# A ring of eight output banks for an MLP, and three instructions of a norm moved behind the next half's sum

## The chip, the cores and the metric

The kernel runs on one core of a Trainium2 chip. The metric is the time of one execution on the device in microseconds; a measurement is the median of several runs.

The engines are TensorE (in the profile PE for products and PEld for loading their weights), VectorE (DVE), ScalarE (ACT), GpSimd (POOL) and the queues that issue transfers. TensorE leaves its results in PSUM, the output memory. It has eight banks, and a product group adds up in one of them until VectorE or ScalarE has read it out.

## The reference, cut to what matters

One inference step of a two-layer decoder trunk on 512 prompt tokens and 8 x 4 sample tokens, in float32. Layer 0 mixes with an mLSTM and a GLA head group, layer 1 with a Mamba-2 SSD mixer; the change touches neither of these two.

```python
def _layernorm(x, g, b):
    xf = x.astype(jnp.float32)
    mu = xf.mean(-1, keepdims=True)
    var = jnp.square(xf - mu).mean(-1, keepdims=True)
    y = (xf - mu) * lax.rsqrt(var + LN_EPS) * g.astype(jnp.float32) + b.astype(jnp.float32)
    return y.astype(x.dtype)

def _mlp(x, w1, w2):
    return jnp.square(jax.nn.relu(x @ w1)) @ w2

for l in range(DEPTH):                      # DEPTH = 2, D_MODEL = 1024, D_FF = 4096
    mix, ... = _ab_mixer(x, ...) if l % 2 == 0 else _ssd_mixer(x, ...)
    x = _layernorm(DN_ALPHA * x + mix, P['ln_mix_g'][l], P['ln_mix_b'][l])
    x = _layernorm(DN_ALPHA * x + _mlp(x, P['mlp_w1'][l], P['mlp_w2'][l]), P['ln_mlp_g'][l], P['ln_mlp_b'][l])
```

## The kernel before, in words

**Layout.** All 544 tokens run together, with features on the 128 partitions and tokens along the free axis: 1024 features are eight tiles (`KT`), the tokens two halves of 272 (`TH`; `hf` is 0 or 1). The stages run in the order `ab`, `mlp0`, `ssd`, `mlp1`, each mixer followed by its output projection, and each projection and each MLP by a norm. The residual stream of a half is `xf[hf]`.

**Products.** A float32 operand is split in a high part (`xh`, `whi`, `hh`, made by ScalarE) and the low remainder (`xl`, `wlo`, `hlo`, made by VectorE). Each 128x128 block of weights takes three products of 272 columns: high by high, high by low, low by high. `dense` (products at L362) adds up one group: one output tile of 128 features for one half, over `kt` blocks, 3 x `kt` products in one bank. Then the evacuation `evac` is issued with high priority. `residual` (L394, L396) is the evacuation that adds a bank to `xf` on VectorE.

**The MLP.** Of the 32 tiles of hidden features the first six (`HEADM`) are dense groups of 24 products. The other 26 are made by `pair`, two tiles for both halves at a time, with seven quarter products instead of eight (Strassen's scheme in Winograd's form): `quarter` issues 12 products at L508, so a pair has 84. A pair uses four banks, of which three are read out and then added to again in the later quarters. The order of pairs and output blocks is the written-out list `MLP`: two output blocks of hidden tiles 0 to 5 (`n` = 6: groups of 18 products), two of hidden tiles 6 and 7 (`n` = 2: eight groups of six products each), then two for every four hidden tiles (eight groups of 12), with a pair after each, and at the end one block of hidden tiles 24 to 31 (`n` = 8).

**Banks before.** There are two sources. `psd` is a pool of three banks, taken in turn; all dense groups use it. `pm` gives the other five, in turn (outside of the SSD layer). A pair takes two from each. The norms' sums over features, `mu` (L420) and `var` (L431), take theirs from `pm`.

**The norm.** `layernorm` runs once for each half, spread between the products: it is a generator in the lane "norm", and each product issued ticks the lane's first generator, which yields how many products it lets pass first (the numbers in `W`). The steps of a half: the sum of its eight tiles of `xf` is made as they are evacuated (L403, L405: on VectorE for the first half; for the second half on GpSimd, the last of them on VectorE). A product with ones makes the mean of it (L420); VectorE removes it (L423), ScalarE squares (L424), VectorE adds the squares up (L425 to L428). Another product makes the variance (L431), ScalarE the reciprocal root (L433, L434). Then for each of eight tiles VectorE scales (L441), ScalarE writes the high part `xh` (L442), VectorE the low part `xl` (L443). Last, ScalarE adds the bias to `xf` in place (L445). The first half's norm runs while TensorE makes the second half's last seven or eight groups of the stage before; the second half's norm while TensorE makes the next stage's first groups, which begin with the first half. A generator behind another in the same lane waits until that one has ended.

**Order on the engines.** TensorE's instructions stand in the order in which the program issues them. For the other engines a planner simulates the kernel's time and lays out each engine's queue ahead of the run, by priority and by when it believes an instruction to be ready. Weight splits (L166 on ScalarE, L167 on VectorE; in the pairs L202, L203) and evacuations have high priority. `tc.issue_after(i)` keeps instructions behind `i` in the queue of `i`'s engine.

**After the first MLP** the SSD layer's first five groups are computed ahead, `xf` is written to memory by GpSimd's queue ("spill") and read again later.

## Time and profile before

| what | value |
| --- | --- |
| median of 3 runs | 1516.64 us (1515.93 to 1519.11) |
| the profiled execution | 1513.8 us, its span 1512.1 us |
| mean granted TensorE clock in the profile | 0.996 |
| `ab` with its projection, to 304 us | TensorE busy 299.06 of 304.00 us |
| `mlp0`, 304 to 678 us | TensorE busy 371.24 of 374.00 us |
| `ssd` with its projection, 678 to 1130 us | TensorE busy 438.45 of 452.00 us |
| `mlp1`, from 1130 us | TensorE busy 369.29 of 382.10 us |

The span is the time from the first to the last instruction in the trace; the rest of the execution lies around it. The times of the views below are microseconds from the span's start. A row of the timeline has start, duration, engine, line, operation, output and inputs, shapes and count, and in brackets the idle time of the engine before it with what ended it.

### The profile page before, as it was taken

What the parts mean: (1) busy time and instruction counts of PE and PEld (TensorE: products, weight loads), DVE (VectorE), ACT (ScalarE), POOL (GpSimd) and SP (SyncE); (2) the same over time, 40 slices, a digit from 0 to 9 for tenths busy, and PEclk for the clock granted to TensorE, in tenths of its full rate; (3) what the DMA queues carried; (4) which work ended last, traced back from release to release, by engine and by line L of the source; (5) the groups of instructions that cost most, each with busy time, mean ns of one, the idle gap of its engine ahead of it and who ended that gap; (6) DMA issues with size and microseconds to landing.
All of it is one profiled execution on the core that took longest, in us unless ns stands there. A gap on an engine that the chain in (4) does not pass through costs nothing.

```text
span 1512.1 us, 29214 instructions
## 1 busy us (share of the span) xinstructions
PE 1478.0 (98%) x11637; PEld 1426.0 (94%) x11637; DVE 1097.9 (73%) x2067; ACT 794.4 (53%) x1748; POOL 230.4 (15%) x295
## 2 busy tenths in 40 slices
PE   9999999999999999999999999999999999999997
PEld 9999989999999999999888789899999999999996
DVE  4956676786776766678898988776688677676656
ACT  5645556573543443447875675554257354344333
POOL 0511221100000000024444354420010000000000
PEclk9999999999999999999999999999999999999999
DMA  6321325223322332433556766364222332233121
GB/s 227 93 68 57 116 85 147 73 71 95 98 90 93 98 87 68 154 128 130 134 178 195 243 169 222 104 211 132 71 74 70 97 96 89 93 99 97 57 85 60
DMA packets 88369, 172.11 MB, mean 114 GB/s; under 512 B 9240, under 2 KB 43928, under 8 KB 87976
## 3 DMA queue, kind: packets, MB, share of 16 engines
q1 hardware_dynamic: 55256, 140.09, 29.7%
q10 hardware_dynamic: 30192, 19.41, 4.8%
q0 software_dynamic: 2784, 10.75, 1.8%
q8 instruction: 91, 1.49, 0.4%
q14 instruction: 46, 0.38, 0.1%
HBM read 153.48 MB, written 16.73 MB: 113 GB/s over the span
## 4 chain that ended last, share of the span: by engine, by line
PE 85%; DVE 6%; ACT 3%; DMA 3%; issue 1%; POOL 1%; ACTq 0%; DVEq 0%; POOLq 0%
PE psd L362 58%; PE psd L508 17%; DMA E<-d_cs 1%; PE num L758 1%; PE yp L1573 1%; PE gs L984 1%; DVE wlo L167 1%; ACT whi L166 1%; PE sp L1551 1%; PE it L1620 1%; DVE xf L396 1%; PE ip L1548 1%; DVE acc L1467 1%; DVE xl L443 1%; PE sps L1627 0%
## 5 line engine op out<-in xcount | busy, mean ns | idle before, releaser
L362 PE MATMUL psd<-xh,whi 128*128 128x272 f32 x1504 | 446.5, 297 | 2.5 <-ACT ci L1457 2.3
L362 PE MATMUL psd<-xh,wlo 128*128 128x272 f32 x1504 | 441.1, 293 | 0.5 <-DVE wlo L167 0.5
L362 PE MATMUL psd<-xl,whi 128*128 128x272 f32 x1504 | 438.3, 291 | 0.2 <-DVE xl L282 0.2
L362 PE MATMUL psd<-hh,whi 128*128 128x272 f32 x1024 | 297.0, 290 | 3.6 <-DVE xf L396 2.5
L362 PE MATMUL psd<-hlo,whi 128*128 128x272 f32 x1024 | 295.5, 289 | 0.2
L362 PE MATMUL psd<-hh,wlo 128*128 128x272 f32 x1024 | 295.2, 288 | 0.0
L362 PEld LDWEIGHTS psd<-xh,whi 128*128 128x128 f32 x1504 | 284.3, 189 | 10.0 <-issue 5.1
L362 PEld LDWEIGHTS psd<-xl,whi 128*128 128x128 f32 x1504 | 284.9, 189 | 5.9 <-issue 4.2
L362 PEld LDWEIGHTS psd<-xh,wlo 128*128 128x128 f32 x1504 | 284.1, 189 | 4.7 <-issue 2.8
L167 DVE TENSOR_TENSOR wlo<-wraw,whi 128x1024 fp32r<-128x1024 f32 (+2 forms) x173 | 206.7, 1196 | 58.4 <-ACT whi L166 57.3
L166 ACT CAST whi<-wraw 128x1024 fp32r<-128x1024 f32 (+2 forms) x173 | 174.2, 1011 | 132.2 <-PE psd L362 114.7
L362 PEld LDWEIGHTS psd<-hh,whi 128*128 128x128 f32 x1024 | 192.8, 188 | 5.7 <-DVE xf L396 4.4
L362 PEld LDWEIGHTS psd<-hlo,whi 128*128 128x128 f32 x1024 | 192.7, 188 | 0.8 <-DVE hlo L282 0.6
L362 PEld LDWEIGHTS psd<-hh,wlo 128*128 128x128 f32 x1024 | 192.7, 188 | 0.1
L396 DVE TENSOR_TENSOR xf<-xf,psd 128x272 f32<-128x272 f32 x208 | 87.9, 432 | 77.3 <-PE psd L362 76.7
L508 PE MATMUL psd<-xh,whi 128*128 128x272 f32 x416 | 120.2, 289 | 0.9 <-DVE xf L396 0.9
L508 PE MATMUL psd<-xh,wlo 128*128 128x272 f32 x416 | 119.9, 288 | 0.0
L508 PE MATMUL psd<-xl,whi 128*128 128x272 f32 x416 | 119.6, 288 | 0.0
L202 ACT CAST whi<-wsum 128x1024 fp32r<-128x1024 f32 x52 | 54.3, 1044 | 120.9 <-PE psd L508 72.0
L202 ACT CAST whi<-wraw 128x1024 fp32r<-128x1024 f32 (+1 forms) x52 | 43.4, 834 | 96.6 <-PE psd L362 85.3
L203 DVE TENSOR_TENSOR wlo<-wsum,whi 128x1024 fp32r<-128x1024 f32 x52 | 63.6, 1224 | 23.1 <-ACT whi L202 23.1
L508 PEld LDWEIGHTS psd<-xh,whi 128*128 128x128 f32 x416 | 78.2, 188 | 1.6 <-DVE xf L396 1.4
(468 smaller groups left out, 2826.5 us busy)
## 6 DMA issues: line engine op xcount, KB each, us to landing
wraw<-mlp_w SPq DMA_DIRECT2D x80, 512.0 KB, 3.6
wraw<-ssd_in SPq DMA_DIRECT2D x40, 512.0 KB, 3.9
wraw<-mlp_w SPq DMA_DIRECT2D x64, 256.0 KB, 2.9
wraw<-ab_in SPq DMA_DIRECT2D x24, 512.0 KB, 3.6
h<-h SPq DMA_DIRECT2D x32, 256.0 KB, 4.4
h0n<-h0n SPq DMA_DIRECT2D x16, 512.0 KB, 4.4
E<-d_cs ACTq DMA_DIRECT2D x16, 512.0 KB, 4.3
s_h<-h0n POOLq DMA_DIRECT2D x16, 512.0 KB, 4.5
```

The costliest lines, as they stand in the source:

```text
L166: nc.scalar.copy(hi[:, r], w[:, r])
L167: nc.vector.tensor_tensor(lo[:, r], w[:, r], hi[:, r].bitcast(F32), ALU.subtract)
L202: self.cut[0] = nc.scalar.copy(hi, x).ins
L203: self.cut[1] = nc.vector.tensor_tensor(lo, x, hi.bitcast(F32), ALU.subtract).ins
L362: last[0] = TE.matmul(ps[:, :TH], wt[:, k, :], rt, start=i == 0, stop=i == n - 1).ins
L396: V.tensor_tensor(x, x, ps, ALU.add)
L443: parts[hf] = V.scalar_tensor_tensor(xl[hf][:, k], xk, b[:, k:k + 1], hi.bitcast(F32), ALU.add, ALU.subtract).ins
L508: last[0] = TE.matmul(ps, wt[:, k], bt[:, k], start=first and n == 0, stop=n == 11, skip_group_check=not first).ins
L758: TE.matmul(num[i], sT[:, i] if j == i else sT[:, (4, 7, 9)[j] + i - j - 1], vt[key][:, j, h, :w], start=j == 0, stop=j == i)
L984: TE.matmul(p[:, 2 * m * b:2 * m * (b + 1)].rearrange("p (e t) -> p e t", e=2), z[:, 2 * m * b:2 * m * b + P], zq[:, :, m * b:m * (b + 1)] ...
L1467: V.scalar_tensor_tensor(acc[:, :n], ci[:, w:w + n], cw[:, m, w:w + 1], acc[:, :n], ALU.mult, ALU.add)
L1548: TE.matmul(ip[:, j * P:(j + 1) * P], hT[:, j * P:(j + 1) * P], Cf[:, tk], start=True, stop=True)
```

## The change

Banks: while an MLP runs (`wide[0]`), `dense` and `pair` take their banks from `bank()`, which goes through `pm` and `psd` in the pattern pm, pm, psd, pm, pm, psd, pm, psd. Since `pm` has five banks and `psd` three, each taken in turn, a bank comes back after eight groups. The norms' `mu` and `var` still take theirs from `pm`. Outside of the MLPs `bank()` gives `psd` as before.

Norms: of the first half's eight low parts (L443) the last three are issued only when the second half's last sum (the L405 on VectorE) has been issued, and are kept behind it in VectorE's queue. The generator waits for that with `need`; the eight bias additions (L445) of that half come behind the low parts in the program. The last norm of the kernel has no low parts and is as before.

```diff
+    wide, at = [False], [0]
+
+    def bank():
+        at[0] += wide[0]
+        return pm("psd") if at[0] % 8 in (1, 2, 4, 5, 7) else psd.tile([P, 512], F32, tag="d", name="psd")
...
     def dense(w, rhs, kt, hf, evac, k0=0, ps=None):
         if ps is None:
-            ps = psd.tile([P, 512], F32, tag="d", name="psd")
+            ps = bank()
...
                 elif m > 1:
-                    E.tensor_tensor(sums[hf], sums[hf], x, ALU.add)
+                    summed = E.tensor_tensor(sums[hf], sums[hf], x, ALU.add).ins
+                    if hf and m == KT - 1:
+                        ready.add(("sum", norms_done[0]))
+                        last_sum[0] = summed
+                        norms_done[0] += 1
...
+        which = norms_done[0] - hf
         yield W["l1" if hf else "l0"]
...
+        def low(k):
+            return V.scalar_tensor_tensor(xl[hf][:, k], x[:, k], b[:, k:k + 1], xh[hf][:, k].bitcast(F32), ALU.add, ALU.subtract).ins
         for k in range(KT):
-            xk, hi = x[:, k], xh[hf][:, k]
+            xk = x[:, k]
             V.scalar_tensor_tensor(xk, xk, g[:, k:k + 1], rs, ALU.mult, ALU.mult)
-            S.activation(hi, xk, AF.Identity, bias=b[:, k:k + 1])
-            parts[hf] = V.scalar_tensor_tensor(xl[hf][:, k], xk, b[:, k:k + 1], hi.bitcast(F32), ALU.add, ALU.subtract).ins
+            S.activation(xh[hf][:, k], xk, AF.Identity, bias=b[:, k:k + 1])
+            if hf or k < KT - 3:
+                parts[hf] = low(k)
+        if not hf:
+            yield from need(("sum", which))
+            with tc.issue_after(last_sum[0]):
+                for k in range(KT - 3, KT):
+                    parts[hf] = low(k)
         for k in range(KT):
             S.activation(x[:, k], x[:, k], AF.Identity, bias=b[:, k:k + 1])
...
         def pair(m):
             w = ws.next()
-            pa, pb, pc, pe = (x[:, :TH] for x in (psd.tile([P, 512], F32, tag="d", name="psd"), pm("psd"),
-                                                  psd.tile([P, 512], F32, tag="d", name="psd"), pm("psd")))
+            pa, pb, pc, pe = (bank()[:, :TH] for _ in range(4))
...
+        wide[0] = True
         phase(HEADM, xrhs, KT, act, head=HEADM)
...
                     mlp(int(stages[n][3]), stages[n], outer, xp, a["yT"] if n + 1 == len(stages) else None)
+                    wide[0], at[0] = False, 0
```

More of the change, by code (lines that the diff above doesn't have):

```diff
@@ L410, in trunk_kernel @@
     parts = [None, None]
+    norms_done, last_sum = [0], [None]
     sums, cut = [None, None], [None, None]
```

## The prediction

> **What bounds the kernel now.** I read the page first: busy shares, then the chain that ended last.
>
> ```profile
> span 1512.1 us, 29214 instructions
> PE 1478.0 (98%) x11637; PEld 1426.0 (94%) x11637; DVE 1097.9 (73%) x2067; ACT 794.4 (53%) x1748; POOL 230.4 (15%) x295
> PE 85%; DVE 6%; ACT 3%; DMA 3%; issue 1%; POOL 1%; ACTq 0%; DVEq 0%; POOLq 0%
> ```
>
> TensorE is busy for 98% of the span and carries 85% of the chain. Neither part of the change removes a product, so all that it can win is idle time of TensorE: 1512.1 - 1478.0 = 34 us in the whole kernel, and little more for the restarts after each pause. Which of it the two parts can reach is told by the view of TensorE's own waits; these are its rows for the MLPs and the norms.
>
> ```profile
> PE mu L420 <- DVE lns L405: 3.4, 2, 3.0
> PE psd L362 <- DVE xf L396: 2.5, 2, 1.3
> PE psd L508 <- DVE xf L396: 0.9, 2, 0.5
> PE psd L362 <- ACT hh L281: 0.7, 2, 0.4
> ```
>
> The columns are total, times, longest. L396 is the addition that empties an output bank into xf: the second and third rows are TensorE waiting for a bank, twice in each row, so once in each MLP. The first row is the norm's mean waiting for the sum of rows on VectorE, 3.0 us once and 0.4 us once. The last row is a product waiting for its operand hh, which no bank changes.
>
> **First part: the banks.** It adds and removes no instruction; it lets a product start when the bank of the eighth group before it is empty, where now it is that of the third. What the waits cost with their restarts I take from the chain, as time from one row to a later one less the undisturbed price of the products between.
>
> ```profile
> 379.21 7.42 PE psd L508 x59
> ...
> 425.99 12.04 PE psd L362 x96
> ...
> 528.57 10.53 PE psd L508 x84
> 539.10 12.09 PE psd L362 x96
> ...
> 561.73 10.55 PE psd L362 x84
> ...
> 574.08 10.53 PE psd L508 x84
> ...
> 1210.72 7.42 PE psd L508 x59
> ...
> 1257.44 12.09 PE psd L362 x96
> ```
>
> The columns are start, duration, what. The undisturbed price is that of a pair and the output block behind it: (10.53 + 12.09) / (84 + 96) = 0.1257 us a product. From 379.21 to 425.99 stand three pairs and two of the short output blocks (k of 2: eight groups of six products): 3 x 84 + 2 x 48 = 348 products, 43.73 us, in 46.78 us: 3.05 us lost. From 561.73 to 574.08 it is one block of 96 products, 12.06 us, in 12.35 us: 0.29 us lost. In the second MLP the stretch from 1210.72 to 1257.44 loses 46.72 - 43.73 = 2.99 us. Sum: 3.05 + 0.29 + 2.99 = 6.3 us. All of it is in blocks whose groups are short: six products are 0.75 us, so the third group before was finished only 1.5 us earlier, and VectorE empties it late because weight splits of 1.2 us stand in its queue.
>
> Would the wait only move? With the bank free, what is late next is VectorE itself. Its load in the first four stretches of that place (short block, pair, short block, pair):
>
> ```profile
> 389.60:397.40 7.80, 6.52 (x50) 6.08 (x48) 7.80 (x17) 3.80 (x10) 0.00 (x0) 1.00 0.34 126
> 397.60:408.00 10.40, 10.40 (x84) 10.40 (x84) 6.21 (x12) 5.52 (x10) 0.00 (x0) 1.00 0.23 55
> 408.20:415.10 6.90, 6.37 (x49) 5.94 (x48) 6.89 (x15) 3.76 (x9) 0.00 (x0) 1.00 0.65 214
> 415.30:425.70 10.40, 10.40 (x83) 10.40 (x84) 6.79 (x13) 4.88 (x10) 0.00 (x0) 1.00 0.20 55
> ```
>
> The columns are the stretch, its length, then busy time (and count) of PE, PEld, DVE, ACT, POOL. In the short blocks VectorE has no free time at all (7.80 of 7.80 us, 6.89 of 6.90), in the pairs behind them it has 4.2 and 3.6 us. TensorE would run 1.8 us ahead in the first block (7.8 us against 48 x 0.1257 = 6.0) and 0.9 us more in the second (6.9 against 6.0): less than the idle time of the pair that follows. So VectorE catches up inside each pair, and the pair's own needs are later still: its first bank to be read back and accumulated into again comes due only with its fifth quarter, 48 products or 6 us after its start. I take the whole 6.3 us; the bounds are nothing gained (VectorE passes all of it on) and 6.3 us; a loss is excluded, since no group waits for a later emptying than before, but for another plan of VectorE's queue (the rivals). I choose the upper end, since the spare 7.8 us exceed the 2.7 us that they must cover. ScalarE, at 3.8 of 7.8 us, is no bound, and these blocks' weights come early: the first 128x1024 split since the MLP's head, which is the first short block's, stands 18 us ahead of it.
>
> ```profile
> 371.17 1.23 DVE L167 TENSOR_TENSOR wlo<-wraw,whi 128x1024 fp32r<-128x1024 f32 x1
> ```
>
> The means of the norms (L420, L431) now take their bank from the ring that the groups use too; the bank that they meet was filled some seven groups before, hence nothing, unless a group of 3 us is emptied over 15 us late.
>
> **Second part: the low parts behind the sum.** In each of the three norms that have low parts (L443; the last norm has none) three of the first half's eight move on VectorE's queue, 9 in all. The first half's last eight ScalarE additions (L445) are issued with them, and in the first MLP's norm the spill of that half, on GpSimd's queue, behind those. In front of the sum stand now, in the norm ahead of the second MLP:
>
> ```profile
> 1125.21 0.49 DVE L443 SCALAR_TENSOR_TENSOR xl<-xf,lnp,xh 128x272 fp32r<-128x272 f32 x1
> 1125.62 0.42 DVE L396 TENSOR_TENSOR xf<-xf,psd 128x272 f32<-128x272 f32 x1
> 1125.97 1.40 DVE L443 SCALAR_TENSOR_TENSOR xl<-xf,lnp,xh 128x272 fp32r<-128x272 f32 x2
> 1127.30 0.42 DVE L396 TENSOR_TENSOR xf<-xf,psd 128x272 f32<-128x272 f32 x1
> 1127.82 0.44 DVE L405 TENSOR_TENSOR lns<-lns,xf 128x272 f32<-128x272 f32 x1
> 1129.08 2.61 DVE L423 SCALAR_TENSOR_TENSOR xf<-mu,xf 128x544 f32<-128x544 f32 x4 [0.82 <-PE mu L420]
> ...
> 1135.30 0.44 DVE L428 TENSOR_TENSOR lnq<-lnq 128x272 f32<-128x272 f32 x1
> ```
>
> ```profile
> 1126.19 0.89 POOL L405 TENSOR_TENSOR lns<-lns,xf 128x272 f32<-128x272 f32 x1 [2.75 <-DVE xf L396]
> ```
>
> ```profile
> 1128.32 0.72 PE L420 MATMUL mu<-lns,ones 128*128 128x272 f32 x2 [3.00 <-DVE lns L405]
> ...
> 1135.91 0.62 PE L431 MATMUL var<-lnq,ones 128*128 128x272 f32 x2
> ```
>
> The three low parts stand ahead of the sum with 0.41 us (1125.21 to 1125.62) and 1.33 us (1125.97 to 1127.30). Without them L396 for the seventh tile runs at 1125.21 and the one for the eighth at 1125.56; now GpSimd's addition of the seventh tile is late next: it starts 0.57 us after its L396 as before, at 1125.78, takes 0.89 us, and the sum starts at 1126.75, the mean at 1127.25 instead of 1128.32: 1.07 us earlier. The low parts then fill 1127.1 to 1128.4, at 0.42 us each, and push the removal of the mean (L423) to 0.42 us after the mean's end (now it starts 0.04 us after it); L428 now ends 0.17 us before the variance (L431) asks for it (1135.74 against 1135.91), so about 0.2 us comes back there. Net 0.85 us. TensorE asks for the first of the low parts (tile 5) with the fifth product behind the mean, no sooner than half the mean and four products after the mean's start: 0.36 + 4 x 0.1257 = 0.86 us, at 1128.1. It is there at 1127.6, and the two others, one 0.42 us and TensorE 0.38 us apart, 0.4 us early. Bounds: all 3.0 us of the wait, if the planner also moves a weight split behind the sum, and a loss (the third rival).
>
> The price of GpSimd's addition carries this term. The same addition took 1.63 us in the other norm (the row below), with which the gain would be 0.33 us. I take 0.89 since VectorE idles while the last one runs. [...]
>
> In the norm between the first MLP and the SSD layer:
>
> ```profile
> 669.24 0.44 DVE L405 TENSOR_TENSOR lns<-lns,xf 128x272 f32<-128x272 f32 x1 [0.33 <-POOL lns L405]
> 669.59 1.22 DVE L167 TENSOR_TENSOR wlo<-wraw,whi 128x1024 fp32r<-128x1024 f32 x1
> 670.73 2.61 DVE L423 SCALAR_TENSOR_TENSOR xf<-mu,xf 128x544 f32<-128x544 f32 x4
> ...
> 676.04 0.44 DVE L428 TENSOR_TENSOR lnq<-lnq 128x272 f32<-128x272 f32 x1
> ```
>
> ```profile
> 667.57 1.63 POOL L405 TENSOR_TENSOR lns<-lns,xf 128x272 f32<-128x272 f32 x1 [1.62 <-DVE xf L396]
> ```
>
> ```profile
> 669.73 0.73 PE L420 MATMUL mu<-lns,ones 128*128 128x272 f32 x2 [0.41 <-DVE lns L405]
> ...
> 677.33 0.62 PE L431 MATMUL var<-lnq,ones 128*128 128x272 f32 x2
> ```
>
> The addition at 667.57 ends at 669.20 and is what the sum waits for; with three low parts fewer ahead it starts over 1 us earlier, and the 0.41 us go, with 0.11 us of restart (the mean's 0.73 us against the variance's 0.62). Against it: the weight split at 669.59 may stay ahead of the low parts, which are then ready 0.1 to 0.2 us after TensorE asks. L428 has 677.33 - 676.48 = 0.85 us of slack. Net 0.4 us. The norm behind the first mixer shows no wait for its sum (the waits' row has two, both told), so nothing is to be had there, and its low parts have as much room as those above. The second half's generator gets its turn one product later (0.13 us), which puts one more product ahead of the mean and costs nothing. The additions L445 move on ScalarE from gaps into gaps: the page's 53% leaves room. The spill and the SSD layer's first GpSimd work move by at most those 3 x 0.43 us; what they feed is hidden behind a whole layer.
>
> **Sum.** 6.3 + 0.85 + 0.4 = 7.6 us off the profiled execution's own 1513.8 us: 1506.2. That execution is 2.8 us under the median of the runs, so for the median I say 1516.64 - 7.6 = 1509.0 us. About 0.2%, 3 us, is what a measurement here can tell from no change.
>
> **Rivals.**
>
> *Half of the banks' gain returns as another wait.* VectorE's order is laid out ahead by a planner's simulation; if in the new order the emptying falls behind the splits, TensorE waits in the pair instead. For it: no idle VectorE in the short blocks. Against: 7.8 us idle right behind. It would give 3.2 + 0.6 = 3.8 us: 1512.8. If all of it returned and the norms won nothing, the change would do nothing: 1516.6.
>
> *The plan changes in a layer that the diff does not touch.* The SSD layer's stretch is where TensorE idles most:
>
> ```profile
> 678.00:1130.00 452.00, 438.45 (x3432) 403.02 (x3431) 368.03 (x663) 271.53 (x685) 154.25 (x202) 0.99 0.51 158
> ```
>
> 13.5 us, 3.0 of them the mean's wait. Half as much again of the other 10.5 would cost 5 us and leave 7.6 - 5 = 2.6 us: 1514.0. For it: its waits are short and many, and the order ahead of it changes at 668 us. Against: its products stay in the same order with the same banks.
>
> *Slower: the low parts come after the removal of the mean and a weight split.* If the planner puts L423 (2.61 us) and a split (1.22 us) ahead of the three low parts, tile 5's low part is ready 0.04 + 2.61 + 0.43 = 3.1 us after the mean's end and the split's 1.1 us later, where TensorE asks 0.14 us after it: 4.0 us late, in three norms 12.0 us. Against 6.3 us from the banks and 1.07 + 0.5 us from the earlier means that is 4.1 us slower: 1520.7. It decides from 7.9 / 3 = 2.6 us of lateness per norm. For it: in the norm ahead of the SSD layer a split already stands between the sum and L423. Against: the low parts are free to go at the sum's end, 0.5 us before the mean is there, and none stands there in the norm ahead of the second MLP.
>
> **How the numbers follow.** The forecast has a chance of 0.60, with a range of its own of 1507.3 to 1512.1 (norms from 0.5 us lost to 3 us won, banks at 5 to 6.3). Half returned 0.12, nothing 0.05, another plan in the SSD layer 0.16, slower 0.07. Faster by over 0.2% is under 1513.6: the forecast nearly whole, most of the half, some of the SSD case: 0.74. Slower 0.09: the slower rival and the bad end of the SSD case. The rest, 0.17, is the same. The range of 1503.5 to 1516.5 goes below by the 2.8 us that one execution stands under the median, with all waits for the sum gone, and above to the case in which nothing is won.
>
> **What would show it.** Right: in TensorE's waits the rows with L396 at L362 and L508 vanish, the short blocks take about 6.0 us instead of 7.9 and 7.0, and the following blocks of 96 stay at 12.1. VectorE stays full in the short blocks. The mean's wait in the norm ahead of the second MLP falls from 3.0 to about 2 us, the other disappears, L443 at L362 gets no row over 0.3 us. Wrong: a new wait of TensorE for xl or whi at those places, or pairs longer than 10.6 us, or more idle time between 678 and 1103 us.

## The result and the profile after

The changed kernel takes 1505.22 us, the median of 7 runs (1499.42 to 1511.98), against 1516.64 us (1512.11 to 1519.49) for the kernel before, measured beside it: a ratio of 0.9926 [0.9900, 0.9953], 0.7% faster. The prediction was 1509.0 us. Its profiled execution took 1500.13 us.

The page after, the rows that answer to those of before (busy time and share, then the shares of the chain that ended last):

```profile
span 1498.4 us, 29214 instructions
PE 1471.6 (98%) x11637; PEld 1422.7 (95%) x11637; DVE 1095.3 (73%) x2067; ACT 794.1 (53%) x1748; POOL 227.8 (15%) x295
PE 87%; DVE 7%; ACT 2%; DMA 2%; issue 1%; POOL 0%; ACTq 0%; SPq 0%; DVEq 0%; POOLq 0%
```

The instructions are the same in number and the span is 13.7 us shorter. TensorE's busy time fell by 6.4 us although it makes the same 11637 products; the loss of waits alone would not do that, and the clock (0.998 granted in the mean of this profile, 0.996 in that of before), further down, has a part in it. TensorE's waits after, for the MLPs and norms (total, times, longest):

```profile
PE mu L431 <- DVE lns L410: 1.6, 1, 1.6
PE var L442 <- DVE lnq L439: 0.2, 1, 0.2
```

L431 is the mean, which was L420; L410 the sum, L442 the variance, L401 the emptying of a bank (was L396). The two rows of waits for L396 at L362 and L508 have no successor. The mean's wait of 3.0 us is 1.6, its other of 0.4 is gone, and there is a new one of 0.2 us at a variance. The chain of after at the blocks that the banks were to speed up (start, duration, what):

```profile
388.94 6.03 PE psd L367 x48
394.97 10.53 PE psd L528 x84
405.50 6.01 PE psd L367 x48
411.51 10.52 PE psd L528 x84
422.03 12.04 PE psd L367 x96
...
1210.63 6.01 PE psd L367 x48
1216.64 10.54 PE psd L528 x84
1227.18 6.01 PE psd L367 x48
1233.18 10.70 PE psd L528 x84
```

Each short block of 48 products takes 6.0 us, where the kernel before took 7.9 and 7.0. The same four stretches of the first MLP by engine (stretch, length, busy time and count of PE, PEld, DVE, ACT, POOL, then the granted clock, which is the share of TensorE's full rate that the profile records, DMA share, GB/s):

```profile
388.80:394.70 5.90, 5.90 (x50) 5.90 (x49) 5.90 (x12) 3.78 (x10) 0.00 (x0) 1.00 0.44 158
394.90:405.20 10.30, 10.30 (x84) 10.30 (x83) 8.13 (x17) 5.62 (x11) 0.00 (x0) 1.00 0.21 56
405.40:411.20 5.80, 5.80 (x48) 5.80 (x48) 5.49 (x12) 3.13 (x8) 0.00 (x0) 1.00 0.79 250
411.40:421.70 10.30, 10.30 (x84) 10.30 (x84) 7.88 (x16) 5.55 (x10) 0.00 (x0) 1.00 0.17 56
```

VectorE still has no free time in the first short block, but 5 of its instructions moved into the pair behind it (17 to 12 there, 12 to 17 here), which keeps 2.2 us free. That is the catching up inside the pair which the prediction had named.

The norm ahead of the second MLP, on VectorE, GpSimd and TensorE (start, duration, engine, line, operation, what, count, and in brackets the idle time before it):

```profile
1114.85 1.21 DVE L167 TENSOR_TENSOR wlo<-wraw,whi 128x1024 fp32r<-128x1024 f32 x1
1115.98 0.77 DVE L401 TENSOR_TENSOR xf<-xf,psd 128x272 f32<-128x272 f32 x2
1117.34 0.44 DVE L410 TENSOR_TENSOR lns<-lns,xf 128x272 f32<-128x272 f32 x1 [0.59 <-POOL lns L410]
1117.70 1.32 DVE L451 SCALAR_TENSOR_TENSOR xl<-xf,lnp,xh 128x272 fp32r<-128x272 f32 x3
1118.94 2.61 DVE L434 SCALAR_TENSOR_TENSOR xf<-mu,xf 128x544 f32<-128x544 f32 x4
...
1124.70 0.43 DVE L439 TENSOR_TENSOR lnq<-lnq 128x272 f32<-128x272 f32 x1
```

```profile
1116.55 0.76 POOL L410 TENSOR_TENSOR lns<-lns,xf 128x272 f32<-128x272 f32 x1 [2.34 <-DVE xf L401]
```

```profile
1117.84 0.50 PE L431 MATMUL mu<-lns,ones 128*128 128x272 f32 x1 [1.62 <-DVE lns L410]
```

The two emptyings now run back to back, the sum waits 0.59 us for GpSimd's addition, and the three low parts (L451) stand directly behind the sum. What still stands ahead of it is a weight split of 1.21 us.

The norm ahead of the SSD layer:

```profile
664.12 0.44 DVE L410 TENSOR_TENSOR lns<-lns,xf 128x272 f32<-128x272 f32 x1
664.48 1.46 DVE L451 SCALAR_TENSOR_TENSOR xl<-xf,lnp,xh 128x272 fp32r<-128x272 f32 x3
665.86 1.21 DVE L167 TENSOR_TENSOR wlo<-wraw,whi 128x1024 fp32r<-128x1024 f32 x1
667.00 2.60 DVE L434 SCALAR_TENSOR_TENSOR xf<-mu,xf 128x544 f32<-128x544 f32 x4
```

```profile
672.80 0.50 PE L442 MATMUL var<-lnq,ones 128*128 128x272 f32 x1 [0.16 <-DVE lnq L439]
```

Behind the sum stand now the low parts (1.46 us) and the split, and the removal of the mean waits for both; the chain of squares behind it ends 0.16 us too late for the variance.

**Where the 13.7 us came from**, by matching the two executions product by product: the places of the bank waits 3.4 us in the first MLP and 3.0 in the second; the norm ahead of the second MLP 1.4; the norm ahead of the SSD layer some 0.3; the kernel's first 15 us 0.7 (the same instructions, other waits for the first weights); and **4.6 us in the SSD layer, which the change does not touch**. The rest, 0.3, is spread thin. So 8.1 us lie where the prediction put 7.6, and the 4.6 us are what the experiments had to explain. A look at the clock gives the first hint. The kernel before, then the kernel after, at places of the SSD layer where TensorE idles most (columns as above; the granted clock is the number ahead of the last two):

```profile
846.70:850.10 3.40, 0.63 (x4) 0.42 (x4) 3.40 (x11) 2.68 (x7) 1.28 (x2) 1.00 0.95 307
850.10:853.50 3.40, 3.15 (x12) 2.48 (x14) 3.40 (x7) 1.80 (x7) 1.29 (x3) 0.50 0.75 289
795.50:798.90 3.40, 1.74 (x10) 0.54 (x8) 3.03 (x10) 2.31 (x8) 0.51 (x4) 1.00 0.51 177
798.90:802.30 3.40, 3.40 (x16) 3.15 (x18) 3.35 (x6) 0.80 (x3) 0.59 (x1) 0.50 1.00 339
```

```profile
836.50:839.90 3.40, 1.71 (x15) 1.43 (x13) 3.40 (x8) 2.03 (x7) 1.34 (x2) 1.00 0.84 286
839.90:843.30 3.40, 2.11 (x16) 1.78 (x18) 3.40 (x9) 3.38 (x12) 1.35 (x2) 1.00 0.81 293
```

Before, two stretches in which TensorE was busy for 0.63 and 1.74 of 3.40 us are each followed by one of the same length at half the clock. After, the pause of the first pair of rows (TensorE's wait at the tile xt, 2.4 us before and 2.2 us here) falls astride two stretches, 1.71 and 2.11 us busy, and none follows at half the clock. By itself a half-rate stretch of 3.41 us at a clock of 0.50 costs up to 3.41 / 2 = 1.7 us, an estimate from these rows: two of them are 3.4 of the 4.6 us, and these rows do not show what the other 1.2 us are.

### The profile page after: what moved, and what is told of

It reads as the page before. It is cut to its first block, busy times and chain, and to the rows that moved or that the text cites. A ratio compares the mean times of both kernels' runs of the same rounds, so it can differ in the third digit from the quotient of the medians.

```text
span 1498.4 us, 29214 instructions
## 1 busy us (share of the span) xinstructions
PE 1471.6 (98%) x11637; PEld 1422.7 (95%) x11637; DVE 1095.3 (73%) x2067; ACT 794.1 (53%) x1748; POOL 227.8 (15%) x295
## 4 chain that ended last, share of the span: by engine, by line
PE 87%; DVE 7%; ACT 2%; DMA 2%; issue 1%; POOL 0%; ACTq 0%; SPq 0%; DVEq 0%; POOLq 0%
PE psd L367 59%; PE psd L528 18%; PE num L778 1%; PE yp L1593 1%; PE gs L1004 1%; DVE acc L1487 1%; DMA h0n<-h0n 1%; DVE wlo L167 1%; PE sp L1571 1%; DVE h0n L1653 1%; PE it L1640 1%; PE ip L1568 1%; ACT whi L166 0%; PE supd L911 0%; PE sps L1647 0%
## 5 line engine op out<-in xcount | busy, mean ns | idle before, releaser
L367 PEld LDWEIGHTS psd<-xh,whi 128*128 128x128 f32 x1504 | 283.5, 188 | 9.3 <-issue 5.1
L367 PEld LDWEIGHTS psd<-xl,whi 128*128 128x128 f32 x1504 | 283.8, 189 | 6.0 <-issue 4.2
L401 DVE TENSOR_TENSOR xf<-xf,psd 128x272 f32<-128x272 f32 x208 | 88.1, 433 | 77.4 <-PE psd L367 76.9
L528 PEld LDWEIGHTS psd<-xl,whi 128*128 128x128 f32 x416 | 78.4, 188 | 0.0
```

What stands on the lines that cost most here:

```text
L367: last[0] = TE.matmul(ps[:, :TH], wt[:, k, :], rt, start=i == 0, stop=i == n - 1).ins
L401: V.tensor_tensor(x, x, ps, ALU.add)
L528: last[0] = TE.matmul(ps, wt[:, k], bt[:, k], start=first and n == 0, stop=n == 11, skip_group_check=not first).ins
```

## The experiments

Theory A: the change is worth what it does in the MLPs and norms, some 8 us; the SSD layer's 4.6 us are chance, set by half-rate stretches. Theory B: the new order ahead of the SSD layer makes that layer quicker, so they belong to the change.

Runs of one kernel differ by 10 us and more. Over all runs of these kernels, the time goes with the mean granted clock of the run: -1.46 us for each 0.001 (standard error 0.07). The price of a half-rate stretch gives about the same: it takes 3.41 x 0.5 / 1510 = 0.0011 off the mean clock and costs up to 1.7 us. So the table gives, beside the ratio, the difference to the kernel before at equal clock, from a fit of all runs with that slope in common (plus or minus two standard errors). The runs come from several chips; a term of its own for each chip moves no row by more than 0.8 us.

| kernel | median us | ratio | at equal clock, us |
| --- | --- | --- | --- |
| after (with `again`) | 1505.22, 1505.35 | 0.9926 [0.9900, 0.9953], 0.9936 [0.9918, 0.9954] | -8.7 ± 1.1 |
| `banks_only` | 1509.33 | 0.9953 [0.9933, 0.9972] | -6.7 ± 1.4 |
| `norms_only` | 1513.28 | 0.9987 [0.9973, 1.0001] | -2.1 ± 1.1 |
| `dense_only` | 1507.24 | 0.9946 [0.9926, 0.9965] | -8.1 ± 1.1 |
| `later_mean` | 1508.52 | 0.9943 [0.9922, 0.9964] | -9.6 ± 1.5 |
| `mixed` | 1506.66 | 0.9940 [0.9915, 0.9965] | -8.0 ± 1.4 |
| `xt_bank` | 1503.65 | 0.9923 [0.9897, 0.9950] | -9.0 ± 1.5 |
| `splits_behind` | 1511.20 | 0.9958 [0.9938, 0.9978] | -8.0 ± 1.1 |
| `filled` | 1511.03 | 0.9966 [0.9948, 0.9983] | -3.6 ± 1.1 |
| `before_filled` | 1520.15 | 1.0033 [1.0014, 1.0052] | +5.0 ± 1.1 |
| `filled_early` | 1507.14 | 0.9935 [0.9912, 0.9958] | -5.9 ± 1.5 |

**The two parts, each alone.** `banks_only` is the changed kernel with the norm's edit undone:

```diff
-            if hf or k < KT - 3:
-                parts[hf] = low(k)
-        if not hf:
-            yield from need(("sum", which))
-            ...
+            parts[hf] = V.scalar_tensor_tensor(xl[hf][:, k], xk, b[:, k:k + 1], hi.bitcast(F32), ALU.add, ALU.subtract).ins
```

> The bank ring alone, the norms as before. Both theories: the short output blocks take 6.0 us each instead of 7.9 and 7.0, TensorE's waits for L396 vanish, the waits for the mean stay at 3.0 and 0.4 us. Theory A (the waits that the two parts remove are the whole effect, about 6.3 us of banks and 1.8 us of norms; what the profile showed beyond that, 4.6 us in the SSD layer and 0.7 us at the start, comes and goes between executions of one and the same kernel): 6.3 us faster, ratio 0.9958. Theory B (the SSD layer is quicker because of the change, 4.6 us): if the bank ring brings that, ratio 0.993.

`norms_only` is the changed kernel with the banks as before:

```diff
-            ps = bank()
+            ps = psd.tile([P, 512], F32, tag="d", name="psd")
...
-            pa, pb, pc, pe = (bank()[:, :TH] for _ in range(4))
+            pa, pb, pc, pe = (x[:, :TH] for x in (psd.tile(...), pm("psd"), psd.tile(...), pm("psd")))
```

> The moved low parts alone, the banks as before. Both theories: the short blocks stay at 7.9 and 7.0 us; the wait for the mean ahead of the second MLP falls from 3.0 to 1.6 us, the one ahead of the SSD layer goes, and the variance there waits 0.2 us. Theory A: 1.8 us faster, ratio 0.9988, not to be told from no change. Theory B, if the norms bring it (the queues' order differs at the SSD layer's start with them): 1.8 + 4.6 = 6.4 us faster, ratio 0.9958.

At equal clock the two parts are worth 6.7 and 2.1 us, together 8.8, and both at once 8.7: they add up within these bounds. In `banks_only` all waits for a bank are gone and the mean's 3.0 and 0.4 us stand; in `norms_only` it is the other way round: the waits for banks stand, with short blocks of 7.91, 6.97, 7.91 and 7.28 us, and of the mean's only 1.6 us are left. The ratio of `norms_only` alone, 0.9987 [0.9973, 1.0001], does not tell it from no change. What Theory A did not expect stands in `banks_only`: with the mean's pause of 3.0 us in place, half the clock follows it, and the 56 products behind the mean take 8.54 us, where the kernel before took 7.03 in its first profile (rows of the chain, the kernel before first; then the stretches of `banks_only` at that place):

```profile
1129.05 7.03 PE psd L362 x56
```

```profile
1122.21 8.54 PE psd L367 x56
```

```profile
1119.50:1122.90 3.40, 1.41 (x9) 1.34 (x10) 2.48 (x6) 1.04 (x2) 0.74 (x1) 1.00 0.33 117
1122.90:1126.30 3.40, 3.40 (x17) 3.40 (x16) 2.69 (x5) 2.67 (x6) 0.00 (x0) 0.50 0.00 0
```

**The same programs again.** `again` is the changed kernel and `before_again` the kernel before, without any edit.

> The changed kernel once more, for the same chip and another profile. Theory A: ratio 0.9946 (8.1 us); the stretch of the SSD layer between the second half's variance before it and the first half's mean behind it (425.3 us before, 420.7 after in the first profiles) comes out anywhere between, by 1.7 us for each window of 3.4 us at half clock that its profile has. Theory B: ratio 0.9915 (12.7 us), and the stretch is 420.7 us again.

> The kernel before, for a second profile. Both theories: short blocks 7.9 and 7.0 us, the mean's waits 3.0 and 0.4 us again. Theory A: the SSD layer's stretch (425.3 us in the first profile) differs by a multiple of about 1.7 us with the number of windows at half clock, and so does the span. Theory B: 425.3 us again, within 0.5.

`again` has a span of 1503.2 us, 4.8 us more than the first profile of the same program, all of it in the SSD layer:

```profile
838.70:842.10 3.40, 1.03 (x10) 0.71 (x8) 3.40 (x11) 2.20 (x5) 0.75 (x1) 1.00 0.82 275
842.10:845.50 3.40, 2.66 (x12) 2.29 (x10) 3.40 (x8) 2.47 (x10) 1.35 (x2) 0.50 0.89 311
845.60:849.00 3.40, 3.40 (x11) 1.74 (x12) 2.95 (x7) 0.43 (x1) 2.01 (x1) 0.51 0.23 40
```

Here the pause falls inside one stretch, 1.03 us of which are busy, and two stretches at half the clock follow. `before_again`, a single run with a span of 1515.3 us, shows the waits of the MLPs again (short blocks of 7.9, 7.1, 7.9 and 7.2 us) and a half-rate stretch behind the mean that the first profile of that kernel lacked:

```profile
1126.40:1129.80 3.40, 0.39 (x5) 0.18 (x3) 3.23 (x7) 1.56 (x3) 0.89 (x1) 1.00 0.43 151
1129.80:1133.20 3.40, 3.40 (x13) 3.17 (x14) 2.10 (x4) 0.66 (x1) 0.00 (x0) 0.50 0.02 5
```

The same program moved by 4.8 us in the layer in question, and the order of VectorE's, ScalarE's and GpSimd's queues in that layer is the same before and after. Above all, the layer takes about the same time before and after when it has as many half-rate stretches. From the start of the second half's variance ahead of it to the start of the first half's mean at its end it took 420.8 us with none (after), 425.7 with two (`again`), 425.6 with two (before), 424.7 with two (`norms_only`) and 427.8 with three (`before_again`); for the first profiles that is within 0.3 us of what the expectation gives. Theory B falls. Theory A's price of 1.7 us was too small: each such stretch came with 2.0 to 2.4 us here, and where the rest goes was not looked for.

**Which of the groups needed the banks?** `dense_only` is the changed kernel with the pairs' four banks taken as before, so that only dense groups go round all eight.

```diff
-            pa, pb, pc, pe = (bank()[:, :TH] for _ in range(4))
+            pa, pb, pc, pe = (x[:, :TH] for x in (psd.tile(...), pm("psd"), psd.tile(...), pm("psd")))
```

> The changed kernel with the pairs' four banks as before (two from each source); the dense groups alone go through the ring of eight. Same queues' orders as the changed kernel. Theory A (what counts is that the groups of six products no longer reuse a bank after three groups): short blocks at 6.0 us, no wait for L396, all of the 6.3 us, ratio to before 0.994 as for the changed kernel. Rival (the pairs' banks count as well: a pair holds two of the three banks of one source until its last quarters, so that the group behind it meets them): up to 0.2 us lost per pair next to a short block, ratio 0.9945 at worst. The two are told apart by the trace alone.

No wait for a bank is left and the short blocks take 6.0 us: at equal clock 8.1 ± 1.1 us against 8.7 ± 1.1. As far as these bounds and the trace tell, the pairs' part of the edit can be left out.

**What is left of the mean's wait.** Three tries. `later_mean` gives the mean of the second half 13 products later in TensorE's order in the norm ahead of the second MLP, and the variance three later in the first MLP's norm:

```diff
-        yield W["l1" if hf else "l0"]
+        yield W["l1" if hf else "l0"] + (13 if hf and i == 2 else 0)
...
-        yield W["v1" if hf else "v0"]
+        yield W["v1" if hf else "v0"] + (3 if hf and i == 1 else 0)
```

> The changed kernel with two of its counts set later: the second half's mean comes 13 products later in the norm ahead of the second MLP, the variance 3 products later in the norm ahead of the SSD layer. TensorE then does products where it now waits 1.6 us for the sum and 0.2 us for the squares. Both theories: these two waits go, 1.6 + 0.3 us less than the changed kernel, no new wait of the second half's products for xl (they have about 1.9 us of room), ratio to before 0.9934 by theory A. If the room is less than it looks, TensorE waits for xl at the second half's first group instead and nothing is won.

Both waits are gone, but TensorE's waits have a new row:

```profile
PE psd L367 <- DVE xl L451: 1.7, 1, 1.7
```

The product that needs the low part of tile 5 stands now ahead of the mean, and that low part is kept behind the sum. The wait has only changed its name. The expectation had named a wait for a low part as its risk, but at the second half's first group. The 9.6 us at equal clock are no more than 8.7 within their bounds.

`mixed` drops the holding back in that one norm, and keeps the mean 13 and the variance three products later as above:

```diff
-            if hf or k < KT - 3:
+            if hf or i == 2 or k < KT - 3:
...
-        if not hf:
+        if not hf and i != 2:
```

> The changed kernel with the norm ahead of the second MLP the other way round: there the low parts stay ahead of the sum and the second half's mean comes 13 products later; in the norm ahead of the SSD layer the variance comes 3 products later. Theory A (in that norm VectorE's queue is late as a whole, so that whatever stands last in it is waited for): TensorE waits for the low parts of tiles 6 and 7, 0.6 and 0.3 us, and no longer for the sum: 0.9 us instead of 1.6, with the variance's 0.3 us a gain of about 1 us over the changed kernel, ratio to before 0.9935. Rival (the sum comes 1 us later than in the changed kernel and the second half's low parts then come too late for its first group): the wait moves there, no gain.

The waits for low parts (0.3 us) and for the mean (0.2 us) are small now, and the trace gains 0.7 us at these two norms; the time does not show it.

`splits_behind` holds two weight blocks of the second MLP back, whose splits stood ahead of the sum, until behind the low parts, and keeps the variance three products later:

```diff
+            if self.limit is not None and self.done >= self.limit:
+                break
...
+        first = next(n for n, b in enumerate(ws.blocks) if b[0] == "mlp1")
+        ws.limit = first + 2
         phase(8, xrhs, KT, residual(False, xp), tail=TAIL, after=lambda hf: launch(layernorm(hf, 2, xp)))
+        ws.limit = None
+        advance(lanes["norm"])
+        for _ in range(2):
+            ws.cut = [None, parts[0]]
+            ws._emit()
```

> The changed kernel, with two weight blocks of the second MLP (the third and fourth of its first weight) split into high and low parts only behind the norm ahead of that MLP, so that VectorE's queue holds about 2.3 us less ahead of the sum of rows; and the first MLP's norm gives its variance step three places later in TensorE's order. Theory A (the mean's wait is the length of VectorE's queue ahead of the sum, and what comes behind the sum can be carried by the pipeline): TensorE's wait of 1.6 us for the mean and that of 0.2 us for the variance in the norm ahead of the SSD layer are gone or below 0.5 us together, no wait above 0.5 us for the delayed blocks' low parts comes in the head of the second MLP, and the time is 1.5 to 2 us below that of the changed kernel at equal granted clock, about 1503.5 us and a ratio of 0.991 to 0.993. Rival (the work is only moved: the delayed splits stand ahead of the low parts or of the scale's products of the norm, and TensorE waits there): the mean's wait is gone, but a wait of 1 to 2 us stands at a low part of the norm or at the delayed blocks' products, and the time is that of the changed kernel at equal clock, a ratio of 0.9935 to 0.995.

The mean waits no more; the variance does (TensorE's waits, then VectorE's queue):

```profile
PE var L445 <- DVE lnq L442: 2.9, 1, 2.9
```

```profile
1121.50 1.32 DVE L454 SCALAR_TENSOR_TENSOR xl<-xf,lnp,xh 128x272 fp32r<-128x272 f32 x3
1122.74 3.48 DVE L168 TENSOR_TENSOR wlo<-wraw,whi 128x1024 fp32r<-128x1024 f32 x3
```

Three splits, 3.48 us, stand ahead of the removal of the mean. The rival held in kind, since the work was only moved, but not in place and size: it looked for 1 to 2 us at a low part or at the delayed blocks. 1.8 us of waits became 2.9, and half the clock follows this pause too:

```profile
1128.80:1132.20 3.40, 0.58 (x5) 0.35 (x3) 3.18 (x6) 1.32 (x3) 0.00 (x0) 1.00 0.06 22
1132.20:1135.60 3.40, 3.34 (x13) 3.13 (x14) 1.07 (x3) 1.99 (x5) 0.00 (x0) 0.50 0.00 0
```

**The SSD layer's pause.** `xt_bank` takes the bank of the first xt of each group of the SSD layer from the other source, since xt waits there for a bank:

```diff
-                p = pm("xt")
+                p = psd.tile([P, 512], F32, tag="d", name="psd") if b == 0 else pm("xt")
```

> The changed kernel with one tile of the SSD layer (xt of the first block of each group) in a bank of the dense groups' source instead of the four others. It is for the longest wait left there, 2.2 to 2.4 us of TensorE at xt for a bank that VectorE has not emptied (L1653), which lies at 840 us, where the profiles of the changed kernel, its repetition, the two halves and the later means show half clock after it or not. Theory A (half clock follows from pauses and is what the executions of one kernel differ by): without that pause fewer windows at half clock at 840 to 860 us, granted clock higher by about 0.001 to 0.002 in the mean of the runs, 2.4 us of wait and 1.7 us for each window that goes: 3 to 6 us less than the changed kernel, ratio to before 0.990 to 0.992. Rival: the dense groups, left with two banks for some us, wait instead, and the clock stays as it is: no change against the changed kernel, 0.994.

xt's wait of 2.2 to 2.4 us is gone, and these came in its place:

```profile
PE sp L1571 <- ACT cb L1546: 2.5, 1, 2.5
PE cb L1534 <- DVE Cf L1493: 2.1, 1, 2.1
```

Its 1503.65 us are the lowest median here, but its interval overlaps that of the changed kernel almost wholly, and at equal clock the two are the same (9.0 against 8.7 us). The mean clock of its runs is 0.9957 against 0.9947, as Theory A wanted, but the wait of 2.4 us was not won. No kernel here is shown to beat the changed one.

**Filling the pause with products.** Three kernels put products of ones by ones, whose results nobody reads, into that pause. The two half-rate stretches in the first profile of the kernel before start 51.20 us apart, 15 times 3.413 us (last section). If the half-rate stretches of an execution lie on such a grid, and TensorE's idle time within a stretch of it decides the clock, the half-rate stretch there must go. `filled` and `before_filled`, the changed kernel and the kernel before:

```diff
+                for _ in range(16 if fill else 0):
+                    TE.matmul(spare_bank[0][:, 2 * P:3 * P], ones, ones, start=True, stop=True)
                 p = pm("xt")
                 ...
+                for _ in range(5 if fill else 0):
+                    TE.matmul(spare_bank[0][:, 2 * P:3 * P], ones, ones, start=True, stop=True)
                 c = pm("cb")
```

> The changed kernel with 21 products of ones by ones, whose results nobody reads, put into TensorE's two pauses in the third group of the SSD layer (16 ahead of the first xt, where every profile so far shows 2.2 to 2.4 us of waiting, and 5 ahead of the cb behind it, 0.5 to 0.8 us), about 0.11 us each. In ten of the eleven profiles shown so far a stretch of 3.41 us at half the granted clock follows a stretch of the same length and grid in which TensorE was busy for 54% or less, and in nine of them this place has one. Theory A (the half-rate stretches are set by TensorE's own idle time within a free-running grid of 3.41 us, and the runs differ by where the grid lies): the pause counts as work now, no half-rate stretch follows at this place (at about 842 to 850 us) in the profile, the mean granted clock of the runs rises by 0.001 to 0.002 and the time falls by 1.5 to 3 us against the changed kernel, to 1502 to 1504 us, a ratio of 0.990 to 0.9925, although 21 products more are made. Rival 1 (the clock falls for another reason, power or load): the half-rate stretch at this place stays, and the time is that of the changed kernel or up to 2 us longer. Rival 2 (the products delay the work behind them): no half-rate stretch, but xt starts later than 2.6 us behind the product ahead, or z and xw stand later in VectorE's queue, and the time is the same or longer.

> The kernel before with the same 21 products in the same two pauses of the SSD layer; neither part of the change is in it. Theory A: it gains the same 1.5 to 3 us against the kernel before, a ratio of 0.998 to 0.999, with a mean granted clock higher by 0.001 to 0.002; its three pauses at output banks and its mean's wait of 3.0 us stay, and with it half-rate stretches right behind that pause in some executions. The difference between this kernel and the changed kernel with the same products is the change itself with less chance in it: 8 to 9.5 us. Theory B (the SSD layer is quicker by the change): the SSD layer of this kernel stays longer than that of the changed kernel with the same products by some 4 us, with other waits than half-rate stretches.

They failed as fillers: at equal clock each is about 5 us slower than the kernel that it is made from. In `filled` the products wait themselves, for the copy out of the bank they write to, and each takes 0.24 us and not 0.11 (a wait's row, then the timeline; 32 passes for 16 products):

```profile
PE Bts L1533 <- ACT Bt L1512: 3.2, 1, 3.2
```

```profile
845.02 3.84 PE L1533 MATMUL Bts<-ones 128*128 128x128 f32 x32 [3.17 <-ACT Bt L1512]
```

The pause is still there, and 5 us of products behind it. But the pair of kernels is a second measure of the change: at equal clock they stand 8.6 us apart (-3.6 against +5.0), as after and before do (8.7). Theory A's 8 to 9.5 us hold once more. Their SSD layers, measured as above, take 430.6 us in both profiles, each with two half-rate stretches, where Theory B looked for some 4 us between them.

`filled_early` puts seven such products ahead of that copy instead, where nothing holds them:

```diff
             TE.transpose(p[:NS, :P], Bf[:, NP:], ident)
+            for _ in range(7 if g == 2 else 0):
+                TE.matmul(p[:, 2 * P:3 * P], ones, ones, start=True, stop=True)
             S.copy(Bt[:NS, 4], p[:NS, :P])
```

> The changed kernel with 7 products of ones by ones, whose results nobody reads, behind the Bts transpose of the SSD layer's third group and ahead of the copy that empties that bank, so that they wait for nothing; by the profile of the last kernel each takes 0.24 us (two passes), 1.7 us in all, of the 2.2 to 2.5 us in which TensorE waits there for the bank of xt. Theory A (half-rate stretches follow from TensorE's idle time within a free-running grid of 3.41 us, from about half of a stretch on): this place keeps at most some 1.5 us of idle time, no half-rate stretch follows it, xt starts as late as without the products, the mean granted clock of the runs lies 0.0005 to 0.002 above that of the changed kernel (0.9947), and the time is 1 to 3 us shorter at best, 1502 to 1505 us, ratio 0.991 to 0.993; at equal clock it is that of the changed kernel within 1.5 us. Rival (the products push other work back, as 21 of them behind the bank's release did): xt or the products that follow start later, and at equal clock the time is 1.5 us or more above the changed kernel, a ratio above 0.994.

```profile
845.90 1.73 PE L1513 MATMUL Bts<-ones 128*128 128x128 f32 x14
848.45 0.63 PE L1534 MATMUL xt<-scon,Y 128*128 128x128 f32 x4 [0.82 <-DVE h0n L1655]
```

```profile
844.50:847.90 3.40, 3.13 (x28) 2.92 (x26) 3.40 (x8) 2.04 (x7) 1.35 (x2) 1.00 0.82 273
847.90:851.30 3.40, 2.09 (x16) 1.76 (x18) 3.40 (x10) 2.67 (x9) 1.39 (x3) 1.00 0.92 294
```

The products take 1.73 us of the pause, 0.82 us remain, and no half-rate stretch follows. The mean clock of its runs is 0.9955 against 0.9947 for the changed kernel, which is more, but no more than such means scatter. The median is 1507.14 us, and at equal clock the kernel is 2.8 ± 1.7 us slower than the changed one. Its SSD layer took 425.9 us with one half-rate stretch elsewhere, where the profiles of `banks_only`, `dense_only` and `mixed` took 423.0 to 424.3 with one. The queues of VectorE, ScalarE and GpSimd stand in another order behind the products; that this is what costs the 2.8 us was not tried. As a reading of the clock the expectation held in this one profile; as to the time the rival did. In one pair of profiles, `filled` and `before_filled`, nearly the same pause lies differently on the grid: 3.17 us, split as 58% and 49% busy in the first, with no half-rate stretch behind it, and with one stretch at 39% in the second, with two behind it.

## Why the prediction was right, and where it was off

**The banks, 6.3 us.** Measured 3.4 + 3.0 = 6.4 us between the two traces, and 6.7 ± 1.4 at equal clock for the banks alone. One term of the sum was not the kernel's: the 0.29 us at the block of 96 at 561.73, whose groups have 12 products and are not short. With the banks of before the same block took 12.06 us in `before_again`, `before_filled` and `norms_only`, so that loss belongs to the one execution that the prediction read, and 6.1 us of the 6.4 to the short blocks with the pairs beside them. The step that VectorE catches up inside the pair held: its load there rose from 6.2 and 6.8 to 8.1 and 7.9 of 10.3 us, and the pairs kept their price but for one of 10.70 us, just above the 10.6 us that the prediction had named as a mark; from start to start the same pair took 10.65 us in the kernel before, so it lost next to nothing. The blocks of 96 stay at 12.04.

**The norm ahead of the second MLP, 0.85 us.** Measured 1.4 us: the mean's wait went from 3.00 to 1.62, where "about 2" was said, and nothing came back. Two terms were off. GpSimd's addition took 0.76 us, with VectorE idle for the 0.59 us ahead of the sum (0.89 taken; the rival price of 1.63 did not come), and the 0.2 us that were to come back at the variance are not there: from the start of the mean's removal (L434) to the end of the last sum of squares (L439) VectorE took 1125.13 - 1118.94 = 6.2 us, where the kernel before took 1135.74 - 1129.08 = 6.7. These two make 0.3 of the 0.5 us between 0.85 and 1.4; the rest is spread over smaller steps. The order behind the sum, low parts first, was as told; the three took 1.32 us there, where two took 1.40 us in the kernel before, while GpSimd's addition of 0.89 us ran.

**The norm ahead of the SSD layer, 0.4 us.** The mean's wait went, but the step "L428 has 0.85 us of slack" fell short: low parts and split together take the time from 664.48 to 667.00, 2.5 us, the variance waits 0.16, and some 0.3 us are left. The prediction looked for the lateness at the low parts, behind the split; the planner put them ahead of it, so the removal of the mean was late instead.

**The norm behind the first mixer, nothing.** So it was.

**The rivals.** Half of the banks' gain did not return as another wait (`banks_only`). The low parts did not come behind the removal of the mean and a split in any norm. The SSD layer's rival named the right place with the wrong cause: it was to change with the plan, for the worse; its queue order did not change, and its time moved with its half-rate stretches, by luck for the better.

**The sum.** 7.6 us were forecast and 8.7 ± 1.1 measured at equal clock. The median fell by more, 11.4 us. 1505.22 us lies below the forecast's own range of 1507.3 to 1512.1. What the sum leaves out is the clock: it takes waits off an execution's time as if only waits set it, while executions of this kernel range from 1507 to 1523 us with their share of half-rate stretches. The raw means of all runs with a recorded clock differ by 10.3 us, of which 0.0011 of mean clock, at 1.46 us per 0.001, is 1.6 us; that difference of clock is itself not told from chance (two standard errors are 0.0012).

**Whether the norm's edit also buys clock** is half shown. In the profiles with a pause of 2.9 to 3.0 us at the norm ahead of the second MLP, a half-rate stretch follows in four of five (not in the first profile of before, where the two stretches were busy for 2.12 and 1.68 us); in the seven with 1.6 us, in none. A pause of 1.6 us takes at most 48% of 3.41 us, one of 3.0 us up to 88%. A half-rate stretch behind the mean costs 1.5 to 1.6 us in the three profiles that have one there (`banks_only`, `before_again`, `before_filled`; the 56 products of `banks_only`: 8.54 against 7.03). But the runs of `norms_only` have the same mean clock as those of before, 0.9936, so the time does not confirm it yet.

## What to carry to other kernels

Look for waits on an output bank where groups are short: here three banks in turn cost 6.1 us at four blocks of groups of six, and at groups of 12 products no more than 0.3 us, in one execution of four. Moving work behind a late sum moves the wait to whatever stands behind it next, so read the queue on both sides of the new place, and stop where the following step's slack is spent. And before a few microseconds in an untouched layer are booked as gain or loss, compare the granted clock of the two executions and profile the same program twice.

## What the runs showed of the hardware

In the first profile of the kernel before, TensorE's granted clock is 0.50, ahead of the last 20 us, in two stretches of 3.41 us, from 798.93 and from 850.13 us: 51.20 us or 15 x 3.413 us apart. In the first profile after there is none but the one at its end, from 1491.84 us, which gives the grid there. How long TensorE was busy in the stretch of 3.4 us ahead: half the clock follows 0.39 us (`before_again`), 0.58 and 1.83 (`splits_behind`), 0.63 and 1.74 (the kernel before), 1.03 (`again`), 1.16 (`filled_early`) and 1.41 (`banks_only`); the full clock follows 1.61 (after, from 720.40 us), 1.71, 1.96 and 2.11 (after), 1.68 and 2.12 (the kernel before) and 2.31 (`again`). Between 1.61 and 1.83 us, 47 to 54% of 3.41, both occur. In the first profiles of before and after, laid whole on their grid from 30 us on and without the last 20 us, no stretch busy for more than 1.75 us has half the clock behind it. In other profiles some have: the one behind 1.83 us above, the second of two half-rate stretches in a row (`again`, behind 2.66 us), and one at about 144 us in two profiles (`later_mean`, `filled_early`), behind a stretch that was wholly busy, for which no cause is known here; in `later_mean` the 12 products from 144.16 us take 3.02 us, in `mixed` 1.70.

Of the pauses of 2.9 to 3.0 us at the norm ahead of the second MLP, four of five have a half-rate stretch behind them, which came with 1.5 to 1.6 us in three profiles; of those of 1.6 us none of seven has one. In the SSD layer each half-rate stretch came with about 2.1 us, from 420.8 us for the layer with none (after) to 429.4 with four (`later_mean`). The longest pause of TensorE in this part of the 14 profiles was 3.17 us (`filled`).
